# Quarter sums of a Winograd product laid out so that plain pairs fill whole PSUM banks, and banks given unit by unit

## The chip, the cores and the metric

One core of one Trainium2 chip runs the whole kernel. The metric is the device time of one execution in microseconds; three runs of the kernel before gave 2130.92, 2132.19 and 2134.03, median 2132.19.

## The reference

Two layers work on a residual stream x of 256 tokens by 2048 features, all in fp32:

```python
for i in range(DEPTH):                      # DEPTH = 2
    h = rms_norm(x, mix_norm_g[i])
    if i % 2 == 0:                          # layer 0: forgetting attention, 16 heads of 128
        mix = fox_attention(h, fox_w_in[j], fox_b_f[j], fox_q_gain[j], fox_k_gain[j], fox_w_out[j])
    else:                                   # layer 1: three dilated windows, 8 heads, values of 256
        mix = dilated_attention(h, dil_w_in[j], dil_q_gain[j], dil_k_gain[j], dil_w_out[j])
    x = x + mix
    h = rms_norm(x, mlp_norm_g[i])
    a = relu(h @ mlp_w_up[i])               # 2048 -> 8192
    x = x + (a * a) @ mlp_w_down[i]         # 8192 -> 2048
```

Nearly all the arithmetic is in products of 256 tokens with weight matrices of 2048 rows or columns; the MLPs hold two thirds of it.

## The kernel before, in words

**Products.** A value in fp32 is kept as a high part, rounded to the fast matmul type, and a low part, the rest. A product is three fast matmuls: high by high, high by low, low by high (`a, h`, `a, l`, `b, h` in the code). Tokens, transposed, are the stationary operand (128 features by 128 tokens); weights move, 512 columns at a time.

**Units.** A `Unit` makes 512 output columns of all 256 tokens from 2048 input features, in eight blocks. A block loads 256 rows of weights (512 KB, one `raw` buffer), cuts them into high (ScalarE, `hi`) and low (VectorE, `lo`), and multiplies its two chunks of 128 rows with the two token tiles: 12 matmuls of 512 columns (`whole`, L384 to L386). There are four `hi` and four `lo` buffers, five of each in an MLP.

**Banks.** PSUM's eight banks are named A0, A1, B0, B1, C0, C1, E0, E1. A plain unit uses a pair of them, one bank for each token tile, and keeps it until its result has been read. Attention heads use C0, C1 (scores, weighted values), E0 and E1 (transposed probabilities).

**Mixed units.** In three of the four periods of each MLP, the up units (24 in all) are mixed: blocks 0, 2, 4, 5 and 7 (`FIVE`) are made by Winograd's variant of Strassen's scheme, with seven products q1 to q7 of 128 by 128 by 256 in place of eight (`parts`, L432 to L434, 21 matmuls of 256 columns). The three others are plain (`quarters`, L403), added directly to the sums that belong to each quarter of the output (token tile t, column half): q3 for (0, 0), q2 for (0, 1), q4 for (1, 1), and a place of its own for (1, 0). Before, four banks A0, A1, C0, C1 hold q1|q5, q2|q6, q7|q4 and q3|(1, 0): no token tile has its two halves in one bank, so a plain pair is 24 matmuls of 256 columns for each of two chunks' twelve. `up_end` then copies the four banks to SBUF (ScalarE, L969: `c` and `z`), adds the sums up on VectorE (L974 to L976, L986, L987), applies relu with the norm's scale (L992), transposes through DRAM (L995, then SP's `blocks` and `mlp_z`) and squares (L1003) into the token tiles `aT`, which the down units use a period later. The six-part buffer `z` is single.

**Order.** The code records operations in a `Plan`, with an engine, an estimated time, and what each reads and writes. Products on TensorE keep the written order. A small simulation of the engines with these estimates gives each of the others a due time, and each engine's instructions are emitted by simulated start. So a changed estimate moves instructions on ScalarE, VectorE and SP. All weight loads and the passes through DRAM are issued by SP in one queue, in that order. Mixed up units alternate block by block with plain down units of the period before.

**Phases.** FoX mixer and its output projection; MLP 0; dilated mixer and its output projection; MLP 1. The first unit of a phase follows the last one of the phase before on TensorE at once. Before, `next_banks()` gives A and B in turn to the units of the mixers, and E to one early unit; up units of the first period take A and B in turn, down units E and B. A unit's result is added to x by `add_to_x` (VectorE, L523), which frees its banks.

Of the kernel before, what the change touches and what calls it, by code (L numbers as in the profile page):

```python
# [17 lines left out]
P = 128  # L18
D = 2048
S = 256  # L20
# [13 lines left out]
N_SLOPES = 3 * DH  # L34

PERIODS = DFF // D
ADDING = ()
FIVE = (0, 2, 4, 5, 7)
MORE = (1, 1, 1)
# [187 lines left out]
def trunk(ctx: ExitStack, tc, x, fox_w_in, fox_b_f, fox_q_gain, fox_k_gain, fox_w_out, dil_w_in,  # L227
# [122 lines left out]
    class Unit:  # L350
# [23 lines left out]
        def whole(self, raw, keys, j, first, last):  # L374
            hi, lo = cut(raw, keys, 0, 2 * NC, j in self.adding)
            for i in range(2):
                k = 2 * j + i

                def go(k=k, i=i):
                    h, l = (in_turn(r(w)[:, i * NC:(i + 1) * NC], NC // 2) for w in (hi, lo))  # L380
                    for t in range(NT):
                        acc = v(self.banks[t])
                        a, b = (self.source.at(k, x, t) for x in range(2))
                        nc.tensor.matmul(acc, a, h, start=first and i == 0, stop=False)  # L384
                        nc.tensor.matmul(acc, a, l, start=False, stop=False)  # L385
                        nc.tensor.matmul(acc, b, h, start=False, stop=last and i == 1)  # L386
                plan.product(6 * 0.216, go, [hi, lo, *self.source.keys(k)], self.banks)

        def quarters(self, raw, keys, j, first, last):
            q = S  # L390
            hi, lo = cut(raw, keys, 0, 2 * NC, j in self.adding)
            for i in range(2):
                k = 2 * j + i

                def go(k=k, i=i):
                    q1q5, q2q6, q7q4, q3 = (v(b) for b in self.banks)
                    to = {(0, 1): q2q6[:, 0:q], (0, 0): q3[:, 0:q], (1, 1): q7q4[:, q:2 * q], (1, 0): q3[:, q:2 * q]}
                    for t in range(NT):
                        a, b = (self.source.at(k, x, t) for x in range(2))
                        for half in range(2):  # L400
                            h, l = (in_turn(r(w)[:, i * NC + half * q:i * NC + (half + 1) * q], P) for w in (hi, lo))
                            for m, w in ((a, h), (a, l), (b, h)):
                                nc.tensor.matmul(to[t, half], m, w, start=False, stop=False)  # L403
                plan.product(12 * 0.109, go, [hi, lo, *self.source.keys(k)], self.banks)

        def parts(self, raw, keys, j, first, last):
            q = S
# [15 lines left out]
            own = lambda i, t: lambda x: self.source.at(2 * j + i, x, t)  # L423

            def go(summing):
                q1q5, q2q6, q7q4, q3 = (v(b) for b in self.banks)
                rows = [[(q1q5[:, 0:q], own(0, 0), pure, 0, 1), (q2q6[:, 0:q], own(1, 0), pure, 2, 1),
                         (q3[:, 0:q], lambda x: at_sigma(x, 3), pure, 1, 3)],
                        [(q1q5[:, q:2 * q], lambda x: at_sigma(x, 0), summed, 0, 2), (q7q4[:, 0:q], lambda x: at_sigma(x, 2), summed, 1, 1),
                         (q2q6[:, q:2 * q], lambda x: at_sigma(x, 1), summed, 2, 2), (q7q4[:, q:2 * q], own(1, 1), summed, 3, 2)]]  # L430
                for acc, a, w, at, edge in rows[summing]:
                    nc.tensor.matmul(acc, a(0), w(0, at), start=first and edge & 1 == 1, stop=False)  # L432
# [451 lines left out]
    AB = [("A0", "A1"), ("B0", "B1")]  # L884
    turn_of = {"n": 0}

    def next_banks():
        turn_of["n"] += 1
        return AB[(turn_of["n"] + 1) % 2]

    AFTER_PAIR = ("E0", "E1")
    for j in range(4):
        got = {}
        sel = selector(j)
# [6 lines left out]

        def v_end(banks):
            got["v"] = values(banks, 0, "fox")
        q_unit, k_unit, v_unit = (fox_unit(col(part, j), AFTER_PAIR if j == 0 and part == 2 else next_banks(), end) for part, end in enumerate((q_end, k_end, v_end)))
        if j == 0:
            for _ in range(4):
                q_unit.blocks(2)
# [8 lines left out]
            go(got["v"])  # L916

    def out_proj(source, w, then):
        units = [Unit(source, w, 0, [(n * NC, NC)], next_banks(), add_to_x(n, then)) for n in range(NX)]
        paired(units[0], units[1])  # L920
        for u in units[2:]:
            u.blocks(NP)
# [20 lines left out]
    def up_end(l, phase, source, halved):  # L943
        own = rings[phase]

        def end(banks):
# [6 lines left out]
                    add("act", on_act(NC), go, reads=[banks[t], f"rstd{l}"], writes=[(z, t)])  # L953
            else:
                c = own["c"].take()
                q1q5, q2q6, q7q4, q3 = banks
# [7 lines left out]
                for b_, to, at, names in pairs:  # L964
                    def go(b_=b_, at=at, names=names):
                        if pure and "22" in names:
                            nc.scalar.copy(at()[:, 0, :].rearrange("p (h n) -> p h n", h=2), v(b_)[:, 0:S].rearrange("p (n h) -> p h n", h=2))
                        else:
                            nc.scalar.copy(flat(at()), two(v(b_)))  # L969
                    add("act", on_act(NC), go, reads=[b_], writes=[(to, x) for x in names])  # L970
# [163 lines left out]
    for _ in range(4):  # L1134
        oD.items.append(aT_ring.take())
    table = tables()
    dil_unit = lambda cols, end, banks=None: Unit(h2, dil_w_in[0], 0, cols, banks or next_banks(), end)
    for q4 in range(4):
        q, k, got = [], [], {}
        units = []  # L1140
        for g in range(3):
            c = g * DH * P + q4 * 2 * P

            def end(banks, g=g):
                qn = turned_heads(banks, 2, "dil")
                q.append(queries(qn, 0, 2, "dil"))
                k.append(keys_of(qn, 2, 2, "dil", DIL_G + 3 + g))
            units.append(dil_unit([(c, 2 * P), (3 * DH * P + c, 2 * P)], end, AFTER_PAIR if q4 == 0 and g == 2 else None))

        def v_end(banks):  # L1150
            got["v"] = values(banks, 2, "dil")
# [21 lines left out]
    def last_by_parts(unit):  # L1173
# [9 lines left out]
        def step(k, part):  # L1183
            t, cols = parts[part]
            hi, lo = cuts[k // 2]
            us = 3 * 0.216 if part == 0 else 3 * 0.109
# [75 lines left out]
```

## Time and profile before

| | us |
|---|---|
| median of three runs | 2132.19 |
| profiled execution, its own time | 2132.55 |
| its span | 2130.8 |
| TensorE busy | 2117.1 (99%) |
| VectorE busy | 1669.3 (78%) |
| ScalarE busy | 1263.0 (59%) |
| DMA, mean rate over the span | 230 GB/s |

A row of the timeline has the start, the duration (both us from the span's start), engine, line, operation and tiles, then the idle time before it and what ended that. Matmuls are pipelined: a row's duration overlaps the next row's, and what a matmul costs in a stream is the distance between starts. In a row of stretches, each engine's busy time and count are followed by the clock granted to TensorE as a share of full speed, the DMA engines' busy share and their rate. Names of tiles stand without buffer numbers, so `hi` is any of four.

### The profile page before, as it was taken

To read this page: it belongs to the slowest core of one execution; us is meant where nothing else is said; L and a number is where in the kernel's file an instruction comes from. 1 tells how busy PE (TensorE), PEld (TensorE's weight loads), DVE (VectorE), ACT (ScalarE), POOL (GpSimd) and SP (SyncE) were. 2 spreads that over 40 slices of the span, in tenths; PEclk is the share of its full clock that TensorE was granted. 3 is DMA by queue.
4 is the path that set the end of the run, shared out by engine and by line. 5 is a ranking of instruction groups with operands and counts; after the bars stand their busy time and mean duration, and the time that the engine had idled before them with its cause. 6 is when DMAs were issued, how large, how long until landed. Compare 5 with 4: busy or idle time off the path is not lost.

```text
span 2130.8 us, 32094 instructions
## 1 busy us (share of the span) xinstructions
PE 2117.1 (99%) x12125; PEld 1917.1 (90%) x12125; DVE 1669.3 (78%) x2092; ACT 1263.0 (59%) x1640; POOL 57.3 (3%) x51
## 2 busy tenths in 40 slices
PE   8999999999999999999999999999999999999999
PEld 7888888899999999998888888888899999999988
DVE  6777777678888898886677777777679888888864
ACT  5555556556666666665456555556666665666652
POOL 1011000000000000000010000000000000000000
PEclk9999999999999999999999999999999999999999
DMA  7776668777677677777686776768767767767773
GB/s 250 236 219 204 214 206 275 229 242 240 219 229 247 227 231 242 235 254 257 214 256 201 235 227 208 244 207 281 237 217 238 246 225 231 248 225 229 247 256 129
DMA packets 336140, 493.04 MB, mean 231 GB/s; under 512 B 21928, under 2 KB 137712, under 8 KB 335984
## 3 DMA queue, kind: packets, MB, share of 16 engines
q1 hardware_dynamic: 335712, 490.86, 71.7%
q8 instruction: 95, 1.56, 0.3%
q14 instruction: 61, 0.50, 0.1%
q10 hardware_dynamic: 272, 0.13, 0.0%
HBM read 455.26 MB, written 35.65 MB: 230 GB/s over the span
## 4 chain that ended last, share of the span: by engine, by line
PE 95%; DMA 2%; DVE 1%; issue 1%; ACT 1%; SPq 0%; DVEq 0%; ACTq 0%
PE bank_B L384 11%; PE bank_B L386 11%; PE bank_B L385 11%; PE bank_A L384 7%; PE bank_A L386 7%; PE bank_A L385 7%; PE bank_C L403 7%; PE bank_E L384 5%; PE bank_E L386 5%; PE bank_E L385 5%; PE bank_A L434 2%; PE bank_A L433 2%; PE bank_A L432 2%; PE bank_A L403 2%; PE bank_C L434 2%; PE bank_C L432 2%
## 5 line engine op out<-in xcount | busy, mean ns | idle before, releaser
L340 ACT CAST hi<-raw 128x1024 fp32r<-128x1024 f32 (+1 forms) x720 | 734.9, 1026 | 618.9 <-PE bank_B L386 211.5
L346 DVE TENSOR_TENSOR lo<-raw,hi 128x1024 fp32r<-128x1024 f32 (+1 forms) x720 | 852.7, 1192 | 295.4 <-ACT hi L340 283.2
L384 PE MATMUL bank_A<-hi,hT 128*128 128x512 f32 x520 | 199.2, 383 | 0.0
L384 PE MATMUL bank_B<-hi,hT 128*128 128x512 f32 x512 | 196.8, 384 | 2.0 <-DVE x L523 2.0
L386 PE MATMUL bank_A<-hi,hT 128*128 128x512 f32 x520 | 197.7, 380 | 0.0
L384 PE MATMUL bank_B<-hi,aT 128*128 128x512 f32 x520 | 197.7, 380 | 0.0
L385 PE MATMUL bank_A<-lo,hT 128*128 128x512 f32 x520 | 197.6, 380 | 0.0
L385 PE MATMUL bank_B<-lo,aT 128*128 128x512 f32 x520 | 197.1, 379 | 0.0
L386 PE MATMUL bank_B<-hi,aT 128*128 128x512 f32 x520 | 197.1, 379 | 0.0
L386 PE MATMUL bank_B<-hi,hT 128*128 128x512 f32 x512 | 194.8, 380 | 0.0
L385 PE MATMUL bank_B<-lo,hT 128*128 128x512 f32 x512 | 194.7, 380 | 0.0
L340 ACT CAST mlp_hi<-raw 128x1024 fp32r<-128x1024 f32 (+1 forms) x108 | 109.6, 1015 | 83.9 <-PE bank_E L386 29.0
L384 PE MATMUL bank_E<-hi,aT 128*128 128x512 f32 x408 | 154.8, 379 | 0.0
L385 PE MATMUL bank_E<-lo,aT 128*128 128x512 f32 x408 | 154.6, 379 | 0.0
L386 PE MATMUL bank_E<-hi,aT 128*128 128x512 f32 x408 | 154.6, 379 | 0.0
L346 DVE TENSOR_TENSOR mlp_lo<-raw,mlp_hi 128x1024 fp32r<-128x1024 f32 (+1 forms) x108 | 126.9, 1175 | 32.8 <-ACT mlp_hi L340 29.7
L403 PE MATMUL bank_C<-hi,hT 128*128 128x256 f32 x672 | 139.9, 275 | 0.0
L403 PEld LDWEIGHTS bank_C<-hi,hT 128*128 128x128 f32 x672 | 115.4, 192 | 1.0
L386 PEld LDWEIGHTS bank_A<-hi,hT 128*128 128x128 f32 x520 | 98.5, 189 | 14.5 <-DVE hT L707 0.5
L384 PEld LDWEIGHTS bank_B<-hi,hT 128*128 128x128 f32 x512 | 97.3, 190 | 15.3 <-issue 2.4
L386 PEld LDWEIGHTS bank_B<-hi,aT 128*128 128x128 f32 x520 | 98.3, 189 | 13.9
L384 PEld LDWEIGHTS bank_A<-hi,hT 128*128 128x128 f32 x520 | 98.8, 190 | 13.2
(360 smaller groups left out, 4723.2 us busy)
## 6 DMA issues: line engine op xcount, KB each, us to landing
raw<-in_mlp_w_up_dram SPq DMA_DIRECT2D x222, 512.0 KB, 4.4
raw<-in_mlp_w_down_dram SPq DMA_DIRECT2D x222, 512.0 KB, 4.7
raw<-in_fox_w_in_dram SPq DMA_DIRECT2D x96, 512.0 KB, 4.5
raw<-in_dil_w_in_dram SPq DMA_DIRECT2D x192, 256.0 KB, 3.0
blocks<-mlp_tr SPq DMA_DIRECT2D x176, 128.0 KB, 3.1
mlp_z<-blocks SPq DMA_DIRECT2D x44, 512.0 KB, 5.6
mlp_raw<-in_mlp_w_up_dram SPq DMA_DIRECT2D x34, 512.0 KB, 5.7
mlp_raw<-in_mlp_w_down_dram SPq DMA_DIRECT2D x34, 512.0 KB, 4.6
```

Source lines behind the costliest of these rows:

```text
L340: add("act", on_act(n), lambda: nc.scalar.copy(r(hi)[:, 0:n], v(src)[:, at:at + n]), reads=keys, writes=[hi])
L346: add("dve", on_dve(n), lambda: nc.vector.tensor_sub(r(lo)[:, 0:n], v(src)[:, at:at + n], v(hi)[:, 0:n]), reads=[*keys, hi], writes=[lo])
L384: nc.tensor.matmul(acc, a, h, start=first and i == 0, stop=False)
L385: nc.tensor.matmul(acc, a, l, start=False, stop=False)
L386: nc.tensor.matmul(acc, b, h, start=False, stop=last and i == 1)
L403: nc.tensor.matmul(to[t, half], m, w, start=False, stop=False)
L432: nc.tensor.matmul(acc, a(0), w(0, at), start=first and edge & 1 == 1, stop=False)
L433: nc.tensor.matmul(acc, a(0), w(1, at), start=False, stop=False)
L434: nc.tensor.matmul(acc, a(1), w(0, at), start=False, stop=last and edge & 2 == 2)
```

## The change

The diff, cut to its core:

```diff
+WHOLE = 6 * 0.2167
+QUARTER = 0.112
...
         def quarters(self, raw, keys, j, first, last):
-            q = S
             hi, lo = cut(raw, keys, 0, 2 * NC, j in self.adding)
+            fresh = j == min(x for x in range(NP) if x not in self.halved)
...
                 def go(k=k, i=i):
-                    q1q5, q2q6, q7q4, q3 = (v(b) for b in self.banks)
-                    to = {(0, 1): q2q6[:, 0:q], (0, 0): q3[:, 0:q], (1, 1): q7q4[:, q:2 * q], (1, 0): q3[:, q:2 * q]}
+                    h, l = (in_turn(r(w)[:, i * NC:(i + 1) * NC], P) for w in (hi, lo))
                     for t in range(NT):
                         a, b = (self.source.at(k, x, t) for x in range(2))
-                        for half in range(2):
-                            h, l = (in_turn(r(w)[:, i * NC + half * q:i * NC + (half + 1) * q], P) for w in (hi, lo))
-                            for m, w in ((a, h), (a, l), (b, h)):
-                                nc.tensor.matmul(to[t, half], m, w, start=False, stop=False)
-                plan.product(12 * 0.109, go, [hi, lo, *self.source.keys(k)], self.banks)
+                        for m, w in ((a, h), (a, l), (b, h)):
+                            to = v(self.banks[2 + t])
+                            if fresh and i == 0 and t == 1 and m is a and w is h:
+                                nc.tensor.matmul(to[:, 0:S], m, w[:, 0:1], start=False, stop=False)
+                                nc.tensor.matmul(to[:, S:], m, w[:, 1:2], start=False, stop=False)
+                            else:
+                                nc.tensor.matmul(to, m, w, start=False, stop=False)
+                plan.product(WHOLE, go, [hi, lo, *self.source.keys(k)], self.banks[2:])
...
-                q1q5, q2q6, q7q4, q3 = (v(b) for b in self.banks)
+                q1q5, q6q7, q3q2, q4 = (v(b) for b in self.banks)
...
-            plan.product(9 * 0.109, lambda: go(0), [hi_w, lo_w, *tok], self.banks)
-            plan.product(12 * 0.109, lambda: go(1), [hi_s, lo_s, *tok], self.banks)
+            plan.product(9 * QUARTER, lambda: go(0), [hi_w, lo_w, *tok], self.banks)
+            plan.product(12 * QUARTER, lambda: go(1), [hi_s, lo_s, *tok], self.banks)
...
+    ROWS_OF_BANKS = {x: (f"{x}0", f"{x}1") for x in "ABE"}
+    fox_banks = [ROWS_OF_BANKS[x] for x in "ABEABABABABA"]
+    dil_banks = [ROWS_OF_BANKS[x] for x in "AEBABABABABABABA"]
+    out_banks = [ROWS_OF_BANKS[x] for x in "BABE"]
...
-                pairs = [(q1q5, c, lambda: c2(), ["c"]), (q2q6, z, lambda: zq()[:, 1:5:3, :], ["11", "u2"]),
-                         (q7q4, z, lambda: zq()[:, 5:2:-2, :], ["u3", "21"]), (q3, z, lambda: zq()[:, 0:3:2, :], ["12", "22"])]
+                for b_, to, at, names in zip(banks, (c, z, z, z), (c2, lambda: zq()[:, 4:6], lambda: zq()[:, 0:2], lambda: zq()[:, 2:4]),
+                                             (["c"], ["u2", "u3"], ["12", "11"], ["22", "21"])):
```

**Quarter sums.** The four banks of a mixed unit now hold q1|q5, q6|q7, q3|q2 and (1, 0)|q4. The last two are the two halves of token tiles 0 and 1, so a plain chunk is six matmuls of 512 columns. The first one that reaches the bank of tile 1 stays split in two, since only one half of that bank has been written by then. TensorE's rows at the first plain chunk of the first mixed unit (tile names with buffer numbers; `hT0` are tokens), before:

```order
L403 MATMUL bank_C_136<-hi3_129,hT0_112 128x256
L403 MATMUL bank_C_136<-lo3_133,hT0_112 128x256
L403 MATMUL bank_C_136<-hi3_129,hT0_112 128x256
L403 MATMUL bank_A_134<-hi3_129,hT0_112 128x256
L403 MATMUL bank_A_134<-lo3_133,hT0_112 128x256
L403 MATMUL bank_A_134<-hi3_129,hT0_112 128x256
L403 MATMUL bank_C_136<-hi3_129,hT0_112 128x256
L403 MATMUL bank_C_136<-lo3_133,hT0_112 128x256
L403 MATMUL bank_C_136<-hi3_129,hT0_112 128x256 x2
```

and now, the chunk's six with the one split:

```order
L407 MATMUL bank_C_136<-hi3_129,hT0_112 128x512
L407 MATMUL bank_C_136<-lo3_133,hT0_112 128x512
L407 MATMUL bank_C_136<-hi3_129,hT0_112 128x512
L404 MATMUL bank_C_136<-hi3_129,hT0_112 128x256
L405 MATMUL bank_C_136<-hi3_129,hT0_112 128x256
L407 MATMUL bank_C_136<-lo3_133,hT0_112 128x512
```

Half as many matmuls of twice the width, all in bank C.

**Banks of units.** Three strings give each unit of the mixers its pair. The FoX units keep theirs. The last unit of both output projections takes E (before: A in layer 0, B in layer 1), the first three units of the dilated mixer A, E, B (before: B, A, E). TensorE's rows from MLP 0's last down unit to the first dilated unit, before:

```order
L385 MATMUL bank_B_135<-mlp0_lo0_2631,aT3_119 128x512
L386 MATMUL bank_B_135<-mlp0_hi0_2630,aT3_119 128x512
L384 MATMUL bank_B_135<-hi0_126,hT0_112 128x512
L385 MATMUL bank_B_135<-lo0_130,hT0_112 128x512
L386 MATMUL bank_B_135<-hi0_126,hT0_112 128x512
```

and now:

```order
L387 MATMUL bank_B_135<-mlp0_lo0_2631,aT3_119 128x512
L388 MATMUL bank_B_135<-mlp0_hi0_2630,aT3_119 128x512
L386 MATMUL bank_A_134<-hi0_126,hT0_112 128x512
L387 MATMUL bank_A_134<-lo0_130,hT0_112 128x512
L388 MATMUL bank_A_134<-hi0_126,hT0_112 128x512
```

The order is the same; the new unit starts in another bank than the one just filled.

**Estimates.** The planner counts 0.2167 us for a wide matmul (before 0.216) and 0.112 for a narrow one (before 0.109). VectorE's rows behind the first mixed unit's sums (`z0` the unit's results, `lo` low parts of weights), before:

```order
L976 TENSOR_TENSOR mlp0_z0_2627<-mlp0_z0_2627 128x256
L986 TENSOR_TENSOR mlp0_z0_2627<-mlp0_z0_2627,mlp0_c0_2628 128x2x256
L987 TENSOR_TENSOR mlp0_z0_2627<-mlp0_z0_2627 128x2x256
L346 TENSOR_TENSOR mlp0_lo0_2631<-raw1_121,mlp0_hi0_2630 128x1024
L346 TENSOR_TENSOR lo0_130<-mlp0_raw0_2629,hi0_126 128x1024
L346 TENSOR_TENSOR lo1_131<-raw2_122,hi1_127 128x768
```

and now:

```order
L975 TENSOR_TENSOR mlp0_z0_2627<-mlp0_z0_2627 128x256
L348 TENSOR_TENSOR mlp0_lo0_2631<-raw1_121,mlp0_hi0_2630 128x1024
L348 TENSOR_TENSOR lo0_130<-mlp0_raw0_2629,hi0_126 128x1024
L348 TENSOR_TENSOR lo1_131<-raw2_122,hi1_127 128x768
L348 TENSOR_TENSOR lo2_132<-raw3_123,hi2_128 128x1024
L348 TENSOR_TENSOR lo3_133<-raw4_124,hi3_129 128x1024
L413 TENSOR_TENSOR mlp0_raw0_2629<-raw1_121 128x512
L985 TENSOR_TENSOR mlp0_z0_2627<-mlp0_z0_2627,mlp0_c0_2628 128x2x256
```

The last two sums of the unit have moved behind five low parts. On SP the unit's pass through DRAM has moved behind two weight loads in the same way. The number of instructions on these engines stays as it was; the copies L969 write other places of `z`.

More of the change, by code (lines that the diff above doesn't have):

```diff
@@ L425, in go @@
             def go(summing):
-                q1q5, q2q6, q7q4, q3 = (v(b) for b in self.banks)
[L427 to L430, printed above, removed]
+                q1q5, q6q7, q3q2, q4 = (v(b) for b in self.banks)
+                rows = [[(q1q5[:, 0:q], own(0, 0), pure, 0, 1), (q3q2[:, q:2 * q], own(1, 0), pure, 2, 1),
+                         (q3q2[:, 0:q], lambda x: at_sigma(x, 3), pure, 1, 2)],
+                        [(q1q5[:, q:2 * q], lambda x: at_sigma(x, 0), summed, 0, 2), (q6q7[:, q:2 * q], lambda x: at_sigma(x, 2), summed, 1, 1),
+                         (q6q7[:, 0:q], lambda x: at_sigma(x, 1), summed, 2, 2), (q4[:, q:2 * q], own(1, 1), summed, 3, 3)]]
                 for acc, a, w, at, edge in rows[summing]:
@@ L903, in v_end @@
             got["v"] = values(banks, 0, "fox")
-        q_unit, k_unit, v_unit = (fox_unit(col(part, j), AFTER_PAIR if j == 0 and part == 2 else next_banks(), end) for part, end in enumerate((q_end, k_end, v_end)))
+        q_unit, k_unit, v_unit = (fox_unit(col(part, j), fox_banks[3 * j + part], end) for part, end in enumerate((q_end, k_end, v_end)))
         if j == 0:
@@ L918, in out_proj @@
     def out_proj(source, w, then):
-        units = [Unit(source, w, 0, [(n * NC, NC)], next_banks(), add_to_x(n, then)) for n in range(NX)]
+        units = [Unit(source, w, 0, [(n * NC, NC)], out_banks[n], add_to_x(n, then)) for n in range(NX)]
         paired(units[0], units[1])
@@ L1136, in trunk @@
     table = tables()
-    dil_unit = lambda cols, end, banks=None: Unit(h2, dil_w_in[0], 0, cols, banks or next_banks(), end)
+    dil_unit = lambda cols, end: Unit(h2, dil_w_in[0], 0, cols, dil_banks.pop(0), end)
     for q4 in range(4):
@@ L1147, in end @@
                 k.append(keys_of(qn, 2, 2, "dil", DIL_G + 3 + g))
-            units.append(dil_unit([(c, 2 * P), (3 * DH * P + c, 2 * P)], end, AFTER_PAIR if q4 == 0 and g == 2 else None))
+            units.append(dil_unit([(c, 2 * P), (3 * DH * P + c, 2 * P)], end))
         def v_end(banks):
@@ L1185, in step @@
             hi, lo = cuts[k // 2]
-            us = 3 * 0.216 if part == 0 else 3 * 0.109
+            us = WHOLE / 2 if part == 0 else 3 * QUARTER
             def go():
```

12 lines of the change are left out of this document (2 added, 10 removed).

## The prediction

> **What bounds the kernel now.** I read the page's busy times and chain first, then the waits of TensorE, then the timeline where each part of the change falls. All sums are made against the profiled execution, 2132.55 us (span 2130.8 and 1.75 around it); the median shown, 2132.19, lies 0.36 lower.
>
> From the page:
>
> ```profile
> span 2130.8 us, 32094 instructions
> PE 2117.1 (99%) x12125; PEld 1917.1 (90%) x12125; DVE 1669.3 (78%) x2092; ACT 1263.0 (59%) x1640; POOL 57.3 (3%) x51
> PE 95%; DMA 2%; DVE 1%; issue 1%; ACT 1%; SPq 0%; DVEq 0%; ACTq 0%
> ```
>
> TensorE has work in 99% of the span, and the chain that ended last runs through it for 95%. So time comes from fewer nanoseconds of TensorE, or from its few waits. Those in the middle of the run are, from the view of waits (us in total, times, longest):
>
> ```profile
> PE bank_B L384 <- DVE x L523: 2.0, 1, 2.0
> PE bank_A L384 <- issue: 1.4, 1, 1.4
> PE bank_A L384 <- ACT aT L642: 0.5, 1, 0.5
> PE bank_C L403 <- DVE mlp_lo L346: 0.2, 1, 0.2
> ```
>
> The first two are at two borders of phases, and the change gives other banks there. VectorE is the nearest second. In a mixed unit of an MLP (columns: stretch, length, then busy time and count for PE, PEld, DVE, ACT, POOL, then granted clock, DMA share, GB/s):
>
> ```profile
> 510.00:551.00 41.00, 41.00 (x280) 38.43 (x279) 35.84 (x44) 25.13 (x31) 0.00 (x0) 1.00 0.72 237
> ```
>
> 35.8 of 41 us: it has 5 us to spare in each unit, which bounds how far a new order may go wrong.
>
> **Term 1: plain pairs as 512-column matmuls.** All instructions of L403 in one window, then TensorE's timeline around one plain pair's first half, and a long run of 512-column matmuls:
>
> ```profile
> 0.00:2131.00 2131.00, 204.87 (x1728) 202.41 (x1728) 1.00 0.72 231
> ```
>
> ```profile
> 463.47 0.28 PE L403 MATMUL bank_C<-hi,hT 128*128 128x256 f32 x1
> ...
> 466.15 0.38 PE L384 MATMUL bank_E<-mlp_hi,aT 128*128 128x512 f32 x1
> ...
> 468.75 0.27 PE L432 MATMUL bank_A<-hi,hT 128*128 128x256 f32 x1
> ```
>
> ```profile
> 1037.40 0.38 PE L386 MATMUL bank_B<-hi,hT 128*128 128x512 f32 x1
> ...
> 1045.82 0.38 PE L386 MATMUL bank_B<-hi,hT 128*128 128x512 f32 x1
> ```
>
> The durations (0.28, 0.38) overlap; the price is the distance of starts. The plain pair is 24 matmuls of 256 columns (two chunks of 12) from 463.47 to 466.15: 2.68/24 = 0.1117 us. The long run has 39 steps in 8.42 us: 0.2159 us for 512 columns. Two narrow ones cost 0.2234, a wide one 0.2159.
>
> The count: 24 mixed units (3 periods, 4 column groups, 2 layers), 3 plain pairs each, 24 matmuls a pair: 1728, the row's number. They become 864 wide ones, less the 24 that stay split in two: 840 wide and 48 narrow. 1728 x 0.1117 = 193.0 us; 840 x 0.2159 + 48 x 0.1117 = 181.4 + 5.4 = 186.7 us. **Gain 6.3 us**, all on the path. The other end of the wide price: 12 wide ones from 466.15 to 468.75, both edges to narrow ones included, make 2.60/12 = 0.2167, and the gain 5.6. I take 6.3, because a step from wide to narrow stands at both ends of such a stretch today too.
>
> The moving operand of the wide form is read in two blocks of 128 interleaved pairs, the narrow one in a single block. Nothing in the trace has that at 512 columns; the nearest is the score matmul L611, read in two blocks at 256 columns, beside the narrow one of L403:
>
> ```profile
> L611 PE MATMUL bank_C<-dil_kl,dil_qh x24: 275/275/275, 1104.0 to 1406.9; 128*128 128x256 f32 x24
> L403 PE MATMUL bank_C<-lo,hT x336: 275/275/275, 463.6 to 2032.7; 128*128 128x256 f32 x168
> ```
>
> Both take 275 ns, so I give the second block no price. The Trainium skill ("TensorE: Matmul & The Clock Gate", Back-to-back issue gap) has N/2.4 + 2.5 ns between warm matmuls: 109.2 and 215.8 ns. It meets the trace for 512 columns and misses it for 256 (0.1117); by it the gain would be 840 x 2.6 ns = 2.2 us, an estimate from that page, and the sum some 4 us poorer. The measured distance decides.
>
> **Term 2: the border from the FoX output projection to the first MLP.** Timeline of TensorE and VectorE:
>
> ```profile
> 376.44 0.38 PE L386 MATMUL bank_A<-hi,aT 128*128 128x512 f32 x1
> 376.85 1.22 DVE L523 TENSOR_TENSOR x<-x,bank_A 128x1024 f32<-128x1024 f32 x1 [0.29 <-PE bank_A L386]
> ...
> 378.18 0.45 PE L384 MATMUL bank_A<-mlp_hi,hT 128*128 128x512 f32 x1 [1.36 <-issue]
> 378.47 0.38 PE L385 MATMUL bank_A<-mlp_lo,hT 128*128 128x512 f32 x1
> ```
>
> The view of waits calls it "issue", but the next matmul writes bank A, and the VectorE add that reads bank A ends at 378.07. With the last unit on E, A was read out long before. From 376.44 to 378.47 lie 2.03 us for two steps of 0.216: **gain 1.6 us**. The add is still made, but nobody on TensorE waits for it. Next in line is the fifth weight block, whose low part VectorE makes after this add (same order before and after):
>
> ```profile
> 379.13 1.22 DVE L346 TENSOR_TENSOR lo<-raw,hi 128x1024 fp32r<-128x1024 f32 x1
> ```
>
> It is done at 380.35; TensorE, starting at 376.66 at 2.59 us a block (12 x 0.2159), needs it at 387.0. The ends are 0 and 1.6; I take 1.6.
>
> **Term 3: the border from the first MLP to the dilated mixer.** VectorE, then TensorE:
>
> ```profile
> 1020.75 1.23 DVE L346 TENSOR_TENSOR lo<-raw,hi 128x1024 fp32r<-128x1024 f32 x1 [1.37 <-ACT hi L340]
> ...
> 1028.35 1.22 DVE L494 TENSOR_TENSOR hT<-mlp_tr,hT 128x1024 fp32r<-128x1024 f32 x1
> 1029.48 1.22 DVE L346 TENSOR_TENSOR lo<-raw,hi 128x1024 fp32r<-128x1024 f32 x1
> 1030.62 1.21 DVE L523 TENSOR_TENSOR x<-x,bank_B 128x1024 f32<-128x1024 f32 x1
> ```
>
> ```profile
> 1029.61 0.38 PE L386 MATMUL bank_B<-mlp_hi,aT 128*128 128x512 f32 x1
> 1031.97 0.45 PE L384 MATMUL bank_B<-hi,hT 128*128 128x512 f32 x1 [1.98 <-DVE x L523]
> ...
> 1036.54 0.38 PE L385 MATMUL bank_B<-lo,hT 128*128 128x512 f32 x1
> ```
>
> ```profile
> 1032.00:1037.00 5.00, 5.00 (x16) 4.10 (x17) 1.44 (x3) 1.86 (x5) 0.70 (x1) 0.66 0.77 203
> 1037.00:1042.00 5.00, 5.00 (x25) 4.38 (x24) 2.45 (x2) 1.83 (x3) 0.00 (x0) 1.00 0.62 198
> ```
>
> TensorE stands still for 1.98 us, and then the granted clock falls: 0.66 over 1032 to 1037, 16 matmuls where the next 5 us hold 25. From 1029.61 to 1036.54 are 14 steps in 6.93 us; at 0.2159 they are 3.02. **Gain 3.9 us**: 2.1 of waiting and 1.8 of slow clock. The change puts the first unit on A, last used by the up units of the last period. Its first four weight blocks have their low parts by 1030.7 (the first from 1020.75, the fourth from 1029.48), while from 1029.83 on one is needed every 2.59 us, the fourth at 1037.6; the tokens made at 1028.35 serve the fifth block. The second unit takes E, emptied when the third down unit was added to x. If the wait went and the slow clock stayed the term would be 2.1, if nothing went 0.
>
> The Trainium skill (the same page, The HAM clock gate) says that the clock halves only after an idle window of about 3.4 us. Here 1.98 us were followed by it; by that rule the wait didn't cause the drop, and the drop might stay.
>
> **Term 4: what the planner moves.** It now counts 0.2167 and 0.112 us a matmul where it counted 0.216 and 0.109, so VectorE, ScalarE and SP get their work in another order in the mixed units. VectorE's last two sums of a unit (L986, L987) move behind five weight cuts. Today they delay one:
>
> ```profile
> 1598.13 0.69 DVE L987 TENSOR_TENSOR mlp_z<-mlp_z 128x512 f32<-128x512 f32 x1
> 1598.74 1.22 DVE L346 TENSOR_TENSOR mlp_lo<-raw,mlp_hi 128x1024 fp32r<-128x1024 f32 x1
> ```
>
> That low part is what L403 waited 0.2 us for; it now comes before them: **gain 0.2 us**. What comes later is the unit's result: on SP its way through DRAM stands behind two more weight loads, one of which goes out for each block, some 2.6 us. Its buffer z must be free when the next unit's banks are copied out. ScalarE and TensorE today:
>
> ```profile
> 497.26 1.09 ACT L969 COPY mlp_z<-bank_C 128x512 f32<-128x512 f32 x2
> 522.98 1.14 ACT L1003 ACTIVATE mlp_tr<-mlp_z 128x512 f32<-128x512 f32 x2
> 536.79 0.58 ACT L969 COPY mlp_c<-bank_A 128x512 f32<-128x512 f32 x1
> ```
>
> ```profile
> 501.62 0.27 PE L432 MATMUL bank_A<-hi,hT 128*128 128x256 f32 x1
> ```
>
> z is read until 524.1 and wanted at 536.8: 12.7 us, of which two loads take 5.2. The banks are empty at 498.35 and wanted at 501.62. The first sums (L974) now need all four copies, not three, but they run after the fourth already. So this costs nothing; cover gone, it is the slower rival below.
>
> The copies keep their number and size, their strides only get plainer, and the plain product no longer naming banks q1q5 and q6q7 frees nothing, since a Winograd pair is first and last in each unit.
>
> **Sum.** 6.3 + 1.6 + 3.9 + 0.2 = 12.0: 2132.55 - 12.0 = 2120.55, and against the median 2120.2. I say 2120.4.
>
> **The rivals.** (a) *New waits in the mixed units*: VectorE is at 87% there, and its queue is in another order. Half a microsecond in 12 of the 24 units gives back 6 us: 2126. For it speaks the wait of 0.2 us that exists; against it, that it is the only one in 24 units. (b) *The slow clock stays at the second border*, because something other than the wait set it: 1.8 us back, 2122.2. Against it, the clock is 1.00 in the stretch behind, and it fell right after the wait. It is what the Trainium skill's rule on the idle window would make of this border. (c) *Another wait takes the place of the bank at the borders*, say the tokens or a late cut: up to 5.5 us back, 2126. Against it, the margins of 6.7 us (387.0 against 380.35) and 6.9 (1037.6 against 1030.7). (d) *The two-block read or the write of a whole bank eats the gain of term 1*: 2126.7. (e) *Slower*: the result's way through DRAM holds z. Margin 12.7 + 3.3 (501.62 against 498.35) = 16.0 us; every us beyond costs one in each of up to 24 units. It decides from a delay of 16.5 us on (12.0/24 = 0.5 above the margin); at 17 us the time is 2144.4. The order moves it by about 5, so I give it little.
>
> **How the numbers follow.** Forecast as summed, within 2 us: 0.68 (2118.5 to 2122.4). (a) 0.12, (b) 0.05, (c) 0.06, (d) 0.04, (e) 0.05. A measurement of this kernel can tell about 0.2%, 4.3 us, from no change: the border is 2127.9. All but (e) and a heavier (a) end below: faster 0.91, same 0.04, slower 0.05. The range goes from 2118.5 (6.5 for term 1 and the 0.5 at L642 gone too) to 2126.5, where (a) and (c) lie; it leaves out (d), (e) and the worse half of (a), some 15 in 100.
>
> **What would show it.** Right: no L403-like narrow matmuls but 48, the wide ones 0.216 apart; no wait of TensorE on x L523 but at the end; granted clock 1.00 through the second border; the matmuls' count near 11285 (12125 - 1728 + 888). Wrong: distances over 0.22 on the wide line (d), a TensorE wait for lo, hi or tokens at a border (c), many waits for lo or mlp_lo in the mixed stretches (a), ScalarE's L969 copies late with TensorE waiting at L436 (e).

## The result, and the profile after

| | before | after |
|---|---|---|
| median, same chip, 4 runs each | 2132.33 | 2121.23 |
| lowest to highest | 2130.92 to 2134.03 | 2120.72 to 2121.26 |
| span of the profiled execution | 2130.8 | 2119.5 |

The ratio is 0.9947, with a 95% interval of 0.9930 to 0.9964: 11.1 us less by the medians. The forecast was 2120.4.

The page of the changed kernel, its span, busy times and the chain that ended last:

```profile
span 2119.5 us, 30432 instructions
PE 2109.8 (100%) x11285; PEld 1888.0 (89%) x11285; DVE 1669.8 (79%) x2092; ACT 1266.0 (60%) x1640; POOL 57.8 (3%) x51
PE 99%; DMA 0%; SPq 0%; DVE 0%; issue 0%; ACT 0%
```

There are 840 matmuls fewer, as counted, and the chain lies on TensorE for 99% where it was 95%. What TensorE still waits for, from the view of waits (us in total, times, longest):

```profile
PE bank_E L701 <- DMA x<-in_x_dram: 2.1, 2, 1.7
PE bank_C L659 <- POOL ident masks.py:199: 1.7, 1, 1.7
PE bank_E L670 <- DMA fox_s<-in_mix_norm_g_dram: 1.3, 1, 1.3
PE bank_B L1191 <- DVE x L1206: 0.8, 1, 0.8
PE bank_B L386 <- ACT aT L646: 0.5, 1, 0.5
```

The first three lie ahead of the first product, the fourth at the very end. Both waits at the borders and the one for `mlp_lo` are gone. One plain pair in TensorE's timeline (the first of its unit, so with the split), and all matmuls of the new wide line in one stretch:

```profile
462.81 0.38 PE L407 MATMUL bank_C<-hi,hT 128*128 128x512 f32 x1
...
463.46 0.27 PE L404 MATMUL bank_C<-hi,hT 128*128 128x256 f32 x1
463.57 0.28 PE L405 MATMUL bank_C<-hi,hT 128*128 128x256 f32 x1
463.69 0.38 PE L407 MATMUL bank_C<-lo,hT 128*128 128x512 f32 x1
...
465.42 0.38 PE L386 MATMUL bank_E<-mlp_hi,aT 128*128 128x512 f32 x1
```

```profile
0.00:2120.00 2120.00, 197.09 (x840) 155.19 (x840) 1.00 0.73 233
```

From 463.69 to 465.42 eight wide matmuls take 1.73 us, 0.216 each, with the weights read in two blocks; the two narrow ones of the split take 0.23. The first border and the second, TensorE's timeline:

```profile
377.38 0.38 PE L388 MATMUL bank_E<-hi,aT 128*128 128x512 f32 x1
377.59 0.38 PE L386 MATMUL bank_A<-mlp_hi,hT 128*128 128x512 f32 x1
...
1025.81 0.38 PE L388 MATMUL bank_B<-mlp_hi,aT 128*128 128x512 f32 x1
1026.02 0.38 PE L386 MATMUL bank_A<-hi,hT 128*128 128x512 f32 x1
```

and the stretch behind the second border (granted clock: the third number from the right):

```profile
1026.00:1031.00 5.00, 5.00 (x25) 4.36 (x24) 3.87 (x5) 2.38 (x5) 0.70 (x1) 1.00 0.70 188
```

The products follow each other at 0.21 to 0.22 us across both borders, and 25 of them lie in the 5 us where there were 16.

Where the time went is read off by holding the same product against itself in both traces. The last product of the FoX output projection starts at 376.44 before and at 377.38 after: the changed kernel is 0.94 us *late* there. The last one of MLP 0 starts at 1029.61 and 1025.81: 3.80 early, so 4.74 came between, 1.60 at the border (2.03 us for two steps have become 0.43) and 3.14 in the mixed units. The second border gives 3.9 (6.93 us for 14 steps, now 25 steps in 5 us). The last matmuls of the program:

```profile
2127.17 0.28 PE L1194 MATMUL bank_A<-mlp_hi,aT 128*128 128x256 f32 x1
```

before, and after:

```profile
2115.87 0.28 PE L1193 MATMUL bank_A<-mlp_hi,aT 128*128 128x256 f32 x1
```

11.30 early at the end. MLP 1 gave the missing 3.6: the 3.1 of its mixed units, and 0.4 to 0.5 at the wait for `mlp_lo`. That wait before:

```profile
1599.57 0.28 PE L403 MATMUL bank_C<-mlp_hi,hT 128*128 128x256 f32 x1
...
1600.23 0.28 PE L403 MATMUL bank_C<-mlp_hi,hT 128*128 128x256 f32 x1
```

Two steps take 0.66 us there where 0.22 is the price, so by the starts it cost 0.44; the 0.2 in the view of waits is only the idle part. The 0.94 was lost at the start. TensorE's first products, before:

```profile
9.51 0.78 PE L384 MATMUL bank_A<-hi,hT 128*128 128x512 f32 x1
...
12.37 0.42 PE L384 MATMUL bank_A<-hi,hT 128*128 128x512 f32 x1
12.63 0.38 PE L385 MATMUL bank_A<-lo,hT 128*128 128x512 f32 x1
```

and after:

```profile
9.25 0.78 PE L386 MATMUL bank_A<-hi,hT 128*128 128x512 f32 x1
...
14.24 0.59 PE L388 MATMUL bank_A<-hi,hT 128*128 128x512 f32 x1
14.67 0.38 PE L386 MATMUL bank_A<-hi,hT 128*128 128x512 f32 x1
```

Products begin 0.26 us sooner, but 12 of them run at half speed (0.427 us apart) where 6 did and a seventh in part. The change alters no operation there. The column of the granted clock says 1.00 for the stretch from 9 to 14 us all the same; the slow products show only in their distances.

### The profile page after: what moved, and what is told of

It is laid out like the page before. It is cut to its first block, busy times and chain, and to the rows that moved or that the text cites. A ratio compares the mean times of both kernels' runs of the same rounds, so it can differ in the third digit from the quotient of the medians.

```text
span 2119.5 us, 30432 instructions
## 1 busy us (share of the span) xinstructions
PE 2109.8 (100%) x11285; PEld 1888.0 (89%) x11285; DVE 1669.8 (79%) x2092; ACT 1266.0 (60%) x1640; POOL 57.8 (3%) x51
## 4 chain that ended last, share of the span: by engine, by line
PE 99%; DMA 0%; SPq 0%; DVE 0%; issue 0%; ACT 0%
PE bank_B L386 11%; PE bank_B L388 11%; PE bank_B L387 11%; PE bank_C L407 9%; PE bank_A L386 7%; PE bank_A L388 7%; PE bank_A L387 7%; PE bank_E L386 7%; PE bank_E L388 7%; PE bank_E L387 7%; PE bank_A L437 3%; PE bank_A L438 3%; PE bank_A L436 3%; PE bank_C L437 2%; PE bank_C L438 2%; PE bank_C L436 2%
## 5 line engine op out<-in xcount | busy, mean ns | idle before, releaser
L386 PE MATMUL bank_A<-hi,hT 128*128 128x512 f32 x552 | 212.0, 384 | 0.0
L388 PE MATMUL bank_A<-hi,hT 128*128 128x512 f32 x552 | 210.3, 381 | 0.0
L387 PE MATMUL bank_A<-lo,hT 128*128 128x512 f32 x552 | 210.2, 381 | 0.0
L386 PE MATMUL bank_B<-hi,hT 128*128 128x512 f32 x480 | 183.7, 383 | 0.0
L387 PE MATMUL bank_B<-lo,hT 128*128 128x512 f32 x480 | 181.9, 379 | 0.0
L388 PE MATMUL bank_B<-hi,hT 128*128 128x512 f32 x480 | 181.9, 379 | 0.0
L386 PE MATMUL bank_E<-hi,aT 128*128 128x512 f32 x472 | 179.0, 379 | 0.0
L387 PE MATMUL bank_E<-lo,aT 128*128 128x512 f32 x472 | 178.9, 379 | 0.0
L388 PE MATMUL bank_E<-hi,aT 128*128 128x512 f32 x472 | 178.9, 379 | 0.0
L407 PE MATMUL bank_C<-hi,hT 128*128 128x512 f32 x430 | 138.5, 379 | 0.0
L388 PEld LDWEIGHTS bank_A<-hi,hT 128*128 128x128 f32 x552 | 104.9, 190 | 15.4 <-DVE hT L711 0.5
L386 PEld LDWEIGHTS bank_A<-hi,hT 128*128 128x128 f32 x552 | 105.1, 190 | 14.0
L387 PEld LDWEIGHTS bank_A<-lo,hT 128*128 128x128 f32 x552 | 105.0, 190 | 14.1
L388 PEld LDWEIGHTS bank_B<-hi,aT 128*128 128x128 f32 x520 | 98.3, 189 | 14.1 <-DVE aT L647 0.2
L386 PEld LDWEIGHTS bank_B<-hi,aT 128*128 128x128 f32 x520 | 98.4, 189 | 13.3 <-ACT aT L646 0.7
```

The lines of the kernel that those rows point to most:

```text
L407: nc.tensor.matmul(to, m, w, start=False, stop=False)
```

## The experiments

### The parts one by one

**Quarter sums alone**: the changed kernel with the banks that the units had before.

```diff
-    dil_banks = [ROWS_OF_BANKS[x] for x in "AEBABABABABABABA"]
-    out_banks = [ROWS_OF_BANKS[x] for x in "BABE"]
+    dil_banks = [ROWS_OF_BANKS[x] for x in "BAEBABABABABABAB"]
+    # out_banks: "BABA" in layer 0, "ABAB" in layer 1
```

> The changed kernel with the old bank of every unit (both borders as before). Theory, the terms of the sum are independent: 2132.3 less 6.3 (wide plain pairs) and about 0.4 (planner order), so 2125.6, 4.4 above the changed kernel, and TensorE waits for the add to x at both borders again. If a wait near 2 us is what brings the slow clock, it follows only where the wait is that long (at the second border 1.98 before; if the add starts sooner now, 1.4 and no slow clock, and the time is nearer 2124). Rival, the wide matmuls bring only the 2.2 us of the page's gap and the rest came from the borders: 2130.

Measured: 2124.65 (2123.34 to 2126.08), ratio 0.9965 (0.9953 to 0.9978) to the kernel before, which ran beside it with a median of 2131.8. That is 7.2 less than before where 6.7 was expected; the rival's 2130 lies outside the runs. The waits of TensorE, and the 5 us behind the second border:

```profile
PE bank_B L386 <- DVE x L527: 2.4, 1, 2.4
PE bank_A L386 <- issue: 1.4, 1, 1.4
PE bank_A L437 <- DVE mlp_lo L348: 0.3, 1, 0.3
```

```profile
1028.00:1033.00 5.00, 3.70 (x10) 3.08 (x11) 2.73 (x5) 1.45 (x4) 0.69 (x1) 0.66 0.77 209
```

Both waits are back, and the slow clock with the longer one. A small wait for `mlp_lo` is there too.

**Bank lists alone**: the kernel before, with the new strings.

```diff
-        units = [Unit(source, w, 0, [(n * NC, NC)], next_banks(), add_to_x(n, then)) for n in range(NX)]
+        units = [Unit(source, w, 0, [(n * NC, NC)], out_banks[n], add_to_x(n, then)) for n in range(NX)]
...
-    dil_unit = lambda cols, end, banks=None: Unit(h2, dil_w_in[0], 0, cols, banks or next_banks(), end)
+    dil_unit = lambda cols, end: Unit(h2, dil_w_in[0], 0, cols, dil_banks.pop(0), end)
```

> The kernel before with the new bank lists alone. Theory: 2132.3 less 1.6 and 3.9 at the borders, 2126.8, with 1728 narrow matmuls of plain pairs still 0.1117 us apart and the clock 1.00 through the second border. Rival, another wait takes the place of the bank once the planner's numbers are the old ones: up to 5.5 back, 2130 to 2132.

Measured: 2127.99 (2126.22 to 2129.66), ratio 0.9982 (0.9973 to 0.9991), 3.8 less than before by the medians and 1.2 above the expectation. In its trace both waits at the borders are gone, and held against the trace before they give 1.6 and 3.9. No other wait took their place there, so that rival falls. What stands against this gain is elsewhere: 0.85 lost at the start, and 0.5 at one wait in the mixed units:

```profile
PE bank_C L403 <- DVE mlp_lo L346: 0.6, 1, 0.6
```

7.2 and 3.8 make 11.0; the changed kernel with the planner's old numbers (the next experiment) lies 10.4 under the same runs of the kernel before. The parts add up within what the runs tell.

**The planner's old numbers** in the changed kernel.

```diff
-WHOLE = 6 * 0.2167
-QUARTER = 0.112
+WHOLE = 6 * 0.216
+QUARTER = 0.109
```

> The changed kernel with the planner's old numbers (0.216 and 0.109 us a matmul). Theory: the order is worth 0.2 to 0.5 us, so 2121.4 to 2121.7. Rival, the new order is what keeps the mixed units free of waits: waits of 0.2 to 0.5 us for low parts return in many of the 24 units, 2123 to 2126.

Measured: 2121.43 (2121.25 to 2121.56), ratio 0.9950 (0.9937 to 0.9962); the changed kernel itself, run again later, had 2121.37. The order differs on VectorE, ScalarE and SP, and no gain from it shows. The wait for `mlp_lo` does not come back either, so the new numbers weren't what removed it.

### Why 256 columns cost more than half of 512

**One plain pair of three in eighths**: 288 matmuls of 512 columns become 1152 of 128.

```diff
+                            elif j == NP // 2 - 1:
+                                for e in range(4):
+                                    nc.tensor.matmul(to[:, e * P:(e + 1) * P], m, w[:, e // 2, e % 2 * (P // 2):(e % 2 + 1) * (P // 2)], start=False, stop=False)
```

> The changed kernel with one of the three plain pairs of every mixed unit cut once more: its 288 matmuls of 512 columns become 1152 of 128. Theory, a matmul that brings its own weights takes at least about 0.11 us however few its columns, which is what the 256-column form paid: 1152 x 0.1117 - 288 x 0.2159 = 66.5 us more, 2187.7. Rival, a matmul costs its columns and a gap (0.0533 + 0.005 us): 1152 x 0.058 - 62.2 = 4.6 us more, 2125.8.

Measured, in one run: 2187.90, 0.2 from the first value and 62 from the second. TensorE's timeline in such a pair (rows with more than one instruction count them at the end):

```profile
474.92 0.61 PE L408 MATMUL bank_C<-lo,hT 128*128 128x128 f32 x4
...
478.05 0.61 PE L408 MATMUL bank_C<-hi,hT 128*128 128x128 f32 x4
```

28 matmuls of this form start from 474.92 up to 478.05 (the last row begins the next four), 0.1118 us apart: a quarter of the columns at half the price of 512. With weights of its own ahead of each matmul a step takes about 0.112 us whether 128 columns follow or 256. So the gain of term 1 is that two steps of this least price (0.2234) became one step for the same columns at 0.2159. What sets the least price, the load of the weights or something else, no run separates: here every matmul brings its own.

### What brings the slow clock at a border

**Longer waits**: the old banks at both borders, and the add to x that TensorE waits for made in two passes.

```diff
-                nc.vector.tensor_add(at, at, v(pair).rearrange("p (t n h) -> p t h n", t=NT, h=2))
+                add_to = v(pair).rearrange("p (t n h) -> p t h n", t=NT, h=2)
+                for t in (1, 1, 0, 0):
+                    nc.vector.scalar_tensor_tensor(at[:, t], add_to[:, t], 0.5, at[:, t], ALU.mult, ALU.add)
```

> The changed kernel with the old banks at both borders, and the add to x that TensorE waits for made there in two passes of half the sum for each token tile (four instructions), so that both waits are about 2.5 us; at the first border it was 1.36 and without a slow clock. Theory, an idle stretch of some 2 us of TensorE is enough to bring the slow clock: at both borders the granted clock falls to about 0.66 in the 5 us behind, 6 or more matmuls 0.43 us apart each. Rival, the drop belongs to the second border whatever the wait, or wants an idle window of 3.4 us as the page has it: none at the first border.

Measured, in one run: 2130.61. The restart at both borders and the 5 us from there:

```profile
380.75 0.46 PE L386 MATMUL bank_A<-mlp_hi,hT 128*128 128x512 f32 x1 [3.02 <-issue]
...
1032.35 0.77 PE L386 MATMUL bank_B<-hi,hT 128*128 128x512 f32 x1 [2.92 <-DVE x L533]
```

```profile
381.00:386.00 5.00, 5.00 (x24) 4.37 (x24) 4.97 (x8) 2.99 (x6) 0.00 (x0) 1.00 0.43 120
1032.00:1037.00 5.00, 4.65 (x11) 3.78 (x12) 1.78 (x4) 1.45 (x4) 0.70 (x1) 0.50 0.49 110
```

The expectation fails: 3.0 us of waiting left the clock alone at the first border, 2.9 halved it at the second, where 1.98 had been enough before. So the length of the wait does not decide by itself. The rival's first form, that the drop belongs to the second border, still stands here (its other form, an idle window of 3.4 us, does not: 2.9 was enough). The run with waits of 4.5 us, below, tests it. The times at which the clock steps up, in the same trace:

```profile
13.99 0.59 PE L387 MATMUL bank_A<-lo,hT 128*128 128x512 f32 x1
14.41 0.38 PE L388 MATMUL bank_A<-hi,hT 128*128 128x512 f32 x1
...
1038.02 0.57 PE L387 MATMUL bank_B<-lo,hT 128*128 128x512 f32 x1
1038.43 0.38 PE L388 MATMUL bank_B<-hi,hT 128*128 128x512 f32 x1
```

Between them lie 1024.02 us. The Trainium skill ("TensorE: Matmul & The Clock Gate", What's actually happening) says that the clock's activity window is 3413 ns long and free-running. This trace agrees: 1024.02 is 300.0 such windows. In the trace before it is 300.0 too (12.45 to 1036.45, both inside a matmul), in that of the quarter sums alone 299.0. Counted on from the step at the start, each idle stretch can be cut at the ends of windows (idle runs from 0.216 after a product's start to the next start; all of it is worked out from the timelines):

| trace, border | idle, us | in one window, in the next | clock behind |
|---|---|---|---|
| before, second | 2.14 | 2.14 | falls |
| quarter sums alone, second | 2.57 | 2.19, 0.38 | falls |
| longer waits, second | 3.09 | 2.33, 0.76 | falls |
| longer waits, first | 3.18 | 2.07, 1.11 | stays |
| before, first | 1.52 | 1.03, 0.50 | stays |

**The same waits, filled**: 22 transposes of the identity in each, written ahead of the first product; their results are thrown away.

```diff
                 def go(k=k, i=i):
+                    if first and i == 0 and self.fill:
+                        wake(22)
```

> As the one with long waits, but TensorE makes 22 transposes of the identity, thrown away, in each of the two waits (some 2.2 of the 2.5 us). Theory, it is TensorE's idling and nothing else at the border that brings the slow clock: the first product still starts 2.5 us late, but at 1.00, and some 1.8 us are gained at each border against the kernel with long waits. Rival, the drop comes from the border (changed data, load on the DMA engines): the clock falls as without the transposes.

Measured, in one run: 2127.51, 3.1 less than the one run without them. TensorE at the second border, and the same 5 us:

```profile
1028.46 2.56 PE L671 MATMUL bank_C<-ident 128*128 128x128 f32 x22
1032.25 0.45 PE L389 MATMUL bank_B<-hi,hT 128*128 128x512 f32 x1 [1.22 <-DVE x L536]
```

```profile
1032.00:1037.00 5.00, 4.75 (x22) 4.22 (x23) 2.49 (x5) 2.49 (x5) 0.70 (x1) 1.00 0.53 124
```

The wait is there, the slow clock is not: 22 matmuls where 11 were. At the first border there was nothing to gain, against the expectation, since the longer wait alone had left the clock up there.

**Waits of 4.5 us**: three passes of a third.

```diff
-                for t in (1, 1, 0, 0):
-                    nc.vector.scalar_tensor_tensor(at[:, t], add_to[:, t], 0.5, at[:, t], ALU.mult, ALU.add)
+                for t in (1, 1, 1, 0, 0, 0):
+                    nc.vector.scalar_tensor_tensor(at[:, t], add_to[:, t], 1 / 3, at[:, t], ALU.mult, ALU.add)
```

> As the one with long waits, but three passes of a third each, so that TensorE idles about 4.5 us at both borders. Theory: what counts is the idling inside one window of 3.413 us, and the clock falls at the window's end where that is about 2.1 us or more (2.14, 2.19 and 2.33 were followed by it, 2.07 was not, though the whole idle stretch was 3.2). 4.5 us leave at least 2.2 in one window wherever its ends fall, so the clock falls at both borders, at the first too, each time at a whole number of windows from the step up at the start. Rival, the first border never brings the slow clock: only at the second.

Measured, in one run: 2133.80. Three us behind the first border as a stretch, and TensorE's restart at the second:

```profile
382.00:385.00 3.00, 3.00 (x8) 2.40 (x8) 2.96 (x6) 1.09 (x4) 0.00 (x0) 0.51 0.01 3
```

```profile
1036.66 0.45 PE L386 MATMUL bank_B<-hi,hT 128*128 128x512 f32 x1 [4.50 <-DVE x L533]
...
1037.17 0.38 PE L388 MATMUL bank_B<-hi,hT 128*128 128x512 f32 x1
1037.39 0.59 PE L386 MATMUL bank_B<-hi,hT 128*128 128x512 f32 x1
1037.77 0.63 PE L387 MATMUL bank_B<-lo,hT 128*128 128x512 f32 x1
```

The clock falls at both borders, so the rival falls, which had the first border as an exception. The windows hold 1.45 and 3.15 us of idling at the first, 2.02 and 2.64 at the second, and the steps up lie 109.0 and 301.0 windows behind the one at the start. The second border shows the most: after 4.5 us of waiting three products still run at full speed, and the clock falls only at 1037.4, where the window with 2.64 us ends (1037.43). The window before it, with 2.02 us, was let pass.

**The kernel before once more.**

> The kernel before once more, for one more position of the windows against the program. Theory: its idling of 2.1 us at the second border brings the slow clock only where it falls into one window nearly whole, in about 4 of 10 executions; whether it does here follows from the step up at the start, counted on in windows of 3.413 us, by the bound of 2.1 us. With the slow clock 16 matmuls lie in 5 us behind the wait, without it 23. Rival, the slow clock follows this wait each time.

Measured, in one run: 2132.74. Some of TensorE's waits:

```profile
PE bank_B L384 <- DVE x L523: 1.4, 1, 1.4
...
PE bank_C L403 <- DVE mlp_lo L346: 1.1, 2, 0.6
```

In this execution the wait at the second border is 1.4, not 2.0 (idle 1.57, all in one window), and no slow clock follows: the low part that stood ahead of the add on VectorE was done in time. So the wait itself changes from one execution to another, which the expectation had not allowed for, and it tells less of the windows than was hoped. It fits the bound, but puts no test between 1.6 and 2.07. In exchange this execution waits for `mlp_lo` twice, loses about 1 us at the start, and its span is the same 2130.8.

### The start

**Eleven thrown-away transposes** in TensorE's idle stretches ahead of the first product.

```diff
+                if n == 0 and pr == 0:
+                    wake(5)
...
+            if name == "mix":
+                wake(6)
```

> The changed kernel with 5 and 6 more transposes of the identity, thrown away, in TensorE's idle stretches at the start (behind the first four transposes of x and behind the one of the gains). Theory, idling at the start is what keeps the clock low for the first matmuls: the 12 matmuls that were 0.43 us apart shrink to 2 or fewer, 2.1 us gained or a little more, 2118.7 to 2119.9. Rival, the clock comes up at a time of its own, or the weights are late next: 2121.2, no change.

Measured: 2120.01 (2119.36 to 2121.78), ratio 0.9944 (0.9932 to 0.9957). Lower than the changed kernel by about 1.4, but with ranges that overlap, and in its trace six products still ran slowly, where two or fewer were expected. That alone decides nothing: the window that ended at 9.20, counted back from the step up, still held two idle pieces, 0.3 and 0.9 us.

**The changed kernel again, and with the start filled up**: 11 transposes at first in place of 8, then 6 and 10.

```diff
-    add("pe", 1.0, lambda: wake(8), writes=["woken"], urgent=True)
+    add("pe", 1.0, lambda: wake(11), writes=["woken"], urgent=True)
...
+                if n == 0 and pr == 0:
+                    wake(6)
...
+            if name == "mix":
+                wake(10)
```

> The changed kernel as it is, beside the next one. Theory from the runs so far: the clock steps only at the ends of windows of 3.413 us that run on through the whole execution and don't start with it (from the step up at the start to the step up at the second border are 300.0, 299.0 and 300.0 windows in the three traces that have both); it steps up behind a window with under some 0.4 us of idling, so at the start between 11.7 and 14.7 us by chance, and the time lies in 2119 to 2122, median 2121.2 less up to a microsecond. Rival, the start is the same in each execution and the spread has another source: all within 0.3 us of 2121.2.

> The changed kernel with 3 more transposes of the identity ahead of x's first and 6 and 10 behind x's first four and behind the one of the gains, so that TensorE idles at most some 0.5 us in one piece from 1.7 us on. Theory: a window without idling ends by 8.5 us, before the first product, no product runs 0.43 us apart, and the time is 1.2 to 2.7 us under the changed kernel's of the same call, 2118.5 to 2119.5, with less spread. Rival, transposes don't count as work for the clock: the step up stays between 11.7 and 14.7, no gain, or a loss of up to 0.5 where a thrown-away transpose is in the way.

Measured, five runs each on the same chip: 2121.37 (2119.97 to 2121.64) and 2119.83 (2119.47 to 2119.90). The ranges don't touch, though by the comparison with the kernel before the two intervals overlap (0.9946, 0.9933 to 0.9960, and 0.9940, 0.9927 to 0.9952). The gain of 1.5 lies in the expected 1.2 to 2.7, the time itself 0.3 above the expected 2119.5. The first transposes of the changed kernel, and then the filled start:

```profile
1.66 1.97 PE L659 MATMUL bank_C<-ident 128*128 128x128 f32 x8 [1.66 <-POOL ident masks.py:199]
```

```profile
6.92 1.31 PE L659 MATMUL bank_C<-ident 128*128 128x128 f32 x10
8.75 0.63 PE L705 MATMUL bank_E<-ident,x 128*128 128x128 f32 x4 [0.52 <-DMA x<-in_x_dram]
9.14 0.46 PE L386 MATMUL bank_A<-hi,hT 128*128 128x512 f32 x1
9.44 0.38 PE L387 MATMUL bank_A<-lo,hT 128*128 128x512 f32 x1
10.03 0.48 PE L388 MATMUL bank_A<-hi,hT 128*128 128x512 f32 x1 [0.21 <-DVE hT L717]
```

Ten transposes take 1.31 us where eight took 1.97, so the clock is up by 6.9, and no product runs slowly. The next thing in line shows at once, 0.2 us for `hT`. It is the fastest kernel of this study, 1.5 us under the changed one. In the changed kernel's second trace the step came at 13.76, in the first at 14.67, both within the 11.7 to 14.7 expected; its runs spread over 1.7 us, those with the filled start over 0.4.

## Why the prediction held, and where it was off

**Term 1** (6.3): right, in place and in size. 3.14 us came in MLP 0's mixed units, so 6.3 in two, and the quarter sums alone gave 7.2 by the medians. (The rows that the prediction calls a pair's first half are the whole pair; its count of 24 is right.) The two-block read costs nothing that shows (0.216), and rival (d) falls. That the measured distance decides for 256 columns is shown by the eighths: a step has a least price of 0.112 us. The Trainium skill ("TensorE: Matmul & The Clock Gate", Back-to-back issue gap) gives 55.8 ns for 128 columns by its formula, which it calls the gap of an isolated matmul, and about 81 ns for a stream with weight loads. Here 111.8 were measured, and the measurement decides.

**Term 2** (1.6): right. The add of x still follows the last product, 0.3 us behind, and nobody waits for it.

**Term 3** (3.9): right for the two traces that were compared, 2.1 of waiting and 1.8 of slow clock, both gone. The step that was mis-sized is to take it for every execution: the kernel before run again waited 1.4 us there with no slow clock. The "gain" at this border is 1.6 in such an execution and up to 3.9 in others, and the profile shown was one of the others. How often the slow clock comes there is open: the mean granted clock is below 1.000 in 8 of 24 runs of the kernel before beside the experiments, but also in 3 of 11 with the new banks alone, whose trace has neither wait.

**Term 4** (0.2): the wait went, and gave 0.4 to 0.5, since its price is 0.44 by the starts and not the 0.2 of idling. The reason was wrong too. "It now comes before them" was put down to the planner's numbers; with the old numbers it goes as well, and with the new ones a wait of 0.3 stands in the trace of the quarter sums alone. Whether the copies in the new layout or the plain products' new form do it was not separated. In the kernel before this wait is not a fixed 0.2 either: another execution has two of up to 0.6.

**The sum.** 12.0 was forecast against the profiled execution, and 11.3 came between the spans. One place is missing in the sum, the start: it has no term because nothing is changed there, yet the two traces differ by 0.94 us for the number of products that ran at half speed. Less by 0.94, more by 0.2 to 0.3 at `mlp_lo`: that is the difference. The time, 2121.2, is 0.8 above the forecast and inside the range from 2118.5 to 2126.5. That it came so close is in part luck: the start alone differs by about 1 us between the two traces of the kernel before, the second border gives 1.6 or 3.9, and five runs of the changed kernel spread over 1.7 us.

**The rivals.** (a) New waits in the mixed units: none in either trace of the changed kernel. The waits of (c) and (e) are in neither trace. (b), the slow clock staying at the second border, did not happen: the wait did cause it, 2.14 us of idling inside one window of 3.41. The Trainium skill ("TensorE: Matmul & The Clock Gate", The HAM clock gate) has the clock fall after an idle window; here a window idle for 2.14 us of 3.41 was enough, and the measurement decides.

## What to carry to other kernels

Where each matmul brings its own weights, count the steps and not only the columns: at 256 columns and at 128 a step cost the same 0.112 us here, so narrow ones that can share a bank are worth making one. A wait of TensorE of about 2 us or more may be charged twice, once as waiting and once as a slow clock behind it, and by chance; give such a border another bank, or, where the wait must stay, fill it with matmuls whose results nobody reads. Before booking a stall out of one trace, look at whether a second execution has it.

## What the hardware showed that was not expected

- The clock's steps lie on a grid that runs through the whole execution: 300.0, 299.0, 300.0, 109.0 and 301.0 windows of 3.413 us between steps up. The position of the grid against the program differs from run to run.
- The clock fell behind windows with 2.14, 2.19, 2.33, 2.64 and 3.15 us of idling, and not behind those with 2.02 and 2.07. The bound lies between 2.07 and 2.14, if these traces are typical. A window with 0.4 us of idling was followed by a step up (the quarter sums alone, second border), one with 0.8 was not (longer waits, second border).
- Transposes of the identity count as work for the clock: they kept it up through a wait of 3.8 us between products, and brought it up ahead of the first one.
- The column of the granted clock does not show the slow products at the start; the distance of their starts, 0.427 us, does.
